# Top-10 indices of each row on one core: instruction order of the schedule versus program order, stores on another queue, loads in four pieces

## The chip, the core and the metric

The kernel runs on one core of one Trainium2 chip. Five instruction streams work on that core side by side: TensorE (not used here), VectorE (DVE in the profile), ScalarE (ACT), GpSimd (POOL) and SyncE (SP). The metric is device time in microseconds, from launch to completion; lower is better. The kernel before has a median of 1136.94 us over 3 runs (1134.1 to 1137.37).

## The reference

For every row of an 8192 x 8192 fp32 matrix it gives the column indices of the 10 largest values, the largest first:

```python
def reference(x, k):                       # x: (8192, 8192) float32, k = 10
    indices = np.argpartition(x, -k, axis=1)[:, -k:]
    values = np.take_along_axis(x, indices, axis=1)
    sorted_idx = np.argsort(-values, axis=1)
    return np.take_along_axis(indices, sorted_idx, axis=1)
```

The matrix is 268 MB and every byte must be read once. The output is 8192 x 10 64-bit integers.

## The kernel before

The rows are cut into 64 tiles of 128 rows, one row in each of the 128 partitions. A row is seen as 256 chunks of 32 values. A tile goes through three stages.

- `load(t)` (L70): SP's queue brings the tile's 4 MB into one of four `xt` buffers, in two DMAs of half the columns each (eight for tile 0).
- `front(t)` (L81): DVE takes the maximum of each chunk (`reduce_max`, L87, one instruction for 8192 elements per partition), then the 8 largest chunk maxima (`max`, L117), their chunk numbers (`max_index`, L118, into `cid`), strikes them out (`match_replace`, L120) and repeats for the next 8 (L122, L123). The 10 largest values of a row lie in the 10 chunks with the largest maxima. So these 10 chunks are fetched again from the matrix in HBM: ACT turns chunk numbers into row offsets (`off`, L104: 8 of them, then 2), and POOL issues 10 indirect DMAs (L109), each of which gathers one chunk of 32 values for all 128 rows into `g`.
- `back(t)` (L127): DVE finds the top 16 among the 320 gathered values with the same five kinds of instruction (L133 to L137) and leaves their positions in `pos`. The first of them, L133, reads all of `g`, and so waits for all 10 gathers. Every eighth tile `decode` (L141) turns the positions of 8 tiles into column indices (six DVE instructions) and stores 80 KB by a DMA on SP's queue (L165).

`cid`, `pos` and the decode's buffers are kept for a batch of `TB = 8` tiles. The buffers of the pool `small` (`m`, `w16`, `m2`, `off`, `g`, ...) rotate over `LAG + 2 = 4` places.

Each engine runs its instructions in the order in which the build put them, and starts one when its semaphores allow it; nothing behind a waiting instruction passes it. What sets that order is the framework's scheduler: it takes the program's dependences and its own cost estimates and may place instructions of different stages between each other. The loop as it is written (L170) calls `load(t)`, `front(t)`, `back(t - 2)` in turn, but the order on DVE is the scheduler's.

Of the kernel before, what the change touches and what calls it, by code (L numbers as in the profile page):

```python
# [10 lines left out]
P = 128  # L11
N = 8192
C = 32
NCHUNK = N // C
KMAX = 10
G = 10
TB = 8
BIG_NEG = -1e30
LAG = 2


@with_exitstack
def kernel(
    ctx: ExitStack,
    tc: tile.TileContext,
    x: bass.AP,
    k: bass.AP,
    out: bass.AP,
):
    nc = tc.nc  # L30
    assert isinstance(k, int) and k == KMAX, f"only k=10 supported, got {k}"
    nrows, rowlen = x.shape
    assert rowlen == N and nrows % (P * TB) == 0, (nrows, rowlen)
    ntiles = nrows // P

    fp32 = mybir.dt.float32
    fp16 = mybir.dt.float16
    u16 = mybir.dt.uint16
    u32 = mybir.dt.uint32
    i32 = mybir.dt.int32  # L40
    X_AX = mybir.AxisListType.X
    ALU = mybir.AluOpType
    ACTF = mybir.ActivationFunctionType

    out_u32 = out.bitcast(u32)
    out_tpn = out_u32.rearrange("(t p) n -> p t n", p=P)

    x_chunks = x.rearrange("r (c w) -> (r c) w", w=C)

    consts = ctx.enter_context(tc.tile_pool(name="consts", bufs=1))  # L50
    xpool = ctx.enter_context(tc.tile_pool(name="x", bufs=4))
    small = ctx.enter_context(tc.tile_pool(name="small", bufs=LAG + 2))
    bpool = ctx.enter_context(tc.tile_pool(name="batch", bufs=2))

    rowbase = consts.tile([P, 1], i32)
    nc.gpsimd.iota(rowbase, pattern=[[0, 1]], base=0, channel_multiplier=NCHUNK)
    rowbase_f = consts.tile([P, 1], fp32)
    nc.vector.tensor_copy(out=rowbase_f, in_=rowbase)
    slots_i = consts.tile([P, G], i32)
    nc.gpsimd.iota(slots_i, pattern=[[1, G]], base=0, channel_multiplier=0)  # L60
    slots = consts.tile([P, G], fp16)
    nc.vector.tensor_copy(out=slots, in_=slots_i)
    opacks = [consts.tile([P, TB, KMAX, 2], u32, name=f"opack{i}") for i in range(2)]
    for o in opacks:
        nc.gpsimd.memset(o, 0)

    st = {}
    batch = {}

    def load(t):  # L70
        xt = xpool.tile([P, N], fp32, tag="xt")
        r0 = t * P
        nparts = 8 if t == 0 else 2
        w = N // nparts
        for h in range(nparts):
            nc.sync.dma_start(
                out=xt[:, h * w:(h + 1) * w], in_=x[r0:r0 + P, h * w:(h + 1) * w]
            )
        st[t] = {"xt": xt}

    def front(t):  # L81
        xt = st[t]["xt"]
        m = small.tile([P, NCHUNK], fp32, tag="m")
        nparts = 8 if t == 0 else 1
        w = N // nparts
        for h in range(nparts):
            nc.vector.reduce_max(  # L87
                out=m[:, h * w // C:(h + 1) * w // C],
                in_=xt[:, h * w:(h + 1) * w].rearrange("p (c w) -> p c w", w=C),
                axis=X_AX,  # L90
            )
        if t % TB == 0:
            batch[t // TB] = (
                bpool.tile([P, TB, 16], u32, tag="cidb", name="cidb"),
                bpool.tile([P, TB, 16], u32, tag="posb", name="posb"),
            )
        cid = batch[t // TB][0][:, t % TB, :]
        w16 = small.tile([P, 16], fp32, tag="w16")
        m2 = small.tile([P, NCHUNK], fp32, tag="m2")
        off = small.tile([P, G], i32, tag="off")  # L100
        g = small.tile([P, G * C], fp32, tag="g")

        def gather(lo, hi):
            nc.scalar.activation(  # L104
                out=off[:, lo:hi], in_=cid[:, lo:hi], func=ACTF.Identity,
                bias=rowbase_f[:, 0:1], scale=1.0,
            )
            for s in range(lo, hi):
                nc.gpsimd.indirect_dma_start(  # L109
                    out=g[:, s * C:(s + 1) * C],  # L110
                    out_offset=None,
                    in_=x_chunks,
                    in_offset=bass.IndirectOffsetOnAxis(ap=off[:, s:s + 1], axis=0),
                    element_offset=t * P * N,
                )

        nc.vector.max(out=w16[:, 0:8], in_=m)  # L117
        nc.vector.max_index(out=cid[:, 0:8], in_max=w16[:, 0:8], in_values=m)  # L118
        gather(0, 8)
        nc.vector.match_replace(out=m2, in_to_replace=w16[:, 0:8], in_values=m,  # L120
                                imm_value=BIG_NEG)
        nc.vector.max(out=w16[:, 8:16], in_=m2)  # L122
        nc.vector.max_index(out=cid[:, 8:16], in_max=w16[:, 8:16], in_values=m2)  # L123
        gather(8, G)
        st[t]["g"] = g

    def back(t):  # L127
        g = st.pop(t)["g"]
        pos = batch[t // TB][1][:, t % TB, :]
        t8a = small.tile([P, 8], fp32, tag="t8a")  # L130
        t8b = small.tile([P, 8], fp32, tag="t8b")
        g2 = small.tile([P, G * C], fp32, tag="g2")
        nc.vector.max(out=t8a, in_=g)  # L133
        nc.vector.max_index(out=pos[:, 0:8], in_max=t8a, in_values=g)  # L134
        nc.vector.match_replace(out=g2, in_to_replace=t8a, in_values=g, imm_value=BIG_NEG)  # L135
        nc.vector.max(out=t8b, in_=g2)  # L136
        nc.vector.max_index(out=pos[:, 8:16], in_max=t8b, in_values=g2)  # L137
        if t % TB == TB - 1:
            decode(t // TB)

    def decode(b):  # L141
        cidb, posb = batch.pop(b)
        slot = bpool.tile([P, TB, KMAX], u32, tag="slot")
        low = bpool.tile([P, TB, KMAX], u32, tag="low")
        nc.vector.tensor_scalar(out=slot, in0=posb[:, :, 0:KMAX], scalar1=C.bit_length() - 1,
                                scalar2=None, op0=ALU.logical_shift_right)
        nc.vector.tensor_scalar(out=low, in0=posb[:, :, 0:KMAX], scalar1=C - 1,
                                scalar2=None, op0=ALU.bitwise_and)
        shape = [P, TB, KMAX, G]
        hot = bpool.tile(shape, fp16, tag="hot")  # L150
        pick = bpool.tile([P, TB, KMAX], fp32, tag="pick")
        nc.vector.tensor_tensor(  # L152
            out=hot, in0=slot.unsqueeze(3).to_broadcast(shape),
            in1=slots.unsqueeze(1).unsqueeze(1).to_broadcast(shape), op=ALU.is_equal,
        )
        nc.vector.tensor_tensor(  # L156
            out=hot, in0=hot, in1=cidb[:, :, 0:G].unsqueeze(2).to_broadcast(shape),
            op=ALU.mult,
        )
        nc.vector.reduce_sum(out=pick, in_=hot, axis=X_AX)  # L160
        o = opacks[b % 2]
        nc.vector.scalar_tensor_tensor(
            out=o[:, :, :, 0], in0=pick, scalar=float(C), in1=low, op0=ALU.mult, op1=ALU.add,
        )
        nc.sync.dma_start(  # L165
            out=out_tpn[:, b * TB:(b + 1) * TB, :],
            in_=o.rearrange("p t k two -> p t (k two)"),
        )

    for t in range(ntiles):  # L170
        load(t)
        front(t)
        if t >= LAG:
            back(t - LAG)
    for t in range(ntiles - LAG, ntiles):
        back(t)


# [33 lines left out]
```

## Time and profile before

| what | value |
|---|---|
| median of 3 runs | 1136.94 us (1134.1 to 1137.37) |
| the profiled execution's own time | 1134.35 us |
| span of its instructions | 1132.6 us |
| DVE busy | 842.8 us (74%) |
| POOL busy | 614.4 us (54%) |
| ACT busy | 39.4 us (3%) |
| moved by DMA | 279.81 MB, mean 247 GB/s over the span |

The time of an execution is 1.75 us more than the span of its instructions. The page gives for each group of instructions its busy time, the mean of one, and the idle time of its engine just before it with what ended that idle time. POOL's busy time is that of issuing gathers, not of their landing. A DMA's time to landing runs from its issue to the semaphore that its waiters see.

### The profile page before, as it was taken

The page shows a single profiled execution, that of the slowest core. Times are in us where ns is not written, and L with a number is a line of the kernel's source. Part 1 is how long each engine was busy: PE and PEld are TensorE (multiplying, and loading weights), DVE is VectorE, ACT ScalarE, POOL GpSimd, SP SyncE. Part 2 cuts the span into 40 slices and gives each one's busy share as a digit, 9 for nine tenths or more (in the row PEclk, how much of TensorE's full clock was granted, in tenths as well). Part 3 has the DMA queues.
Part 4 walks back from the last instruction along what each step waited for, and adds up shares of the span by engine and source line. Part 5 has one row for each costly group of instructions (what it writes and reads, how often), then busy time and mean ns, then how long its engine had stood idle before and what let it go on. Part 6 is the DMA issues. An engine that isn't in the chain of part 4 may idle for free.

```text
span 1132.6 us, 2913 instructions
## 1 busy us (share of the span) xinstructions
DVE 842.8 (74%) x1145; ACT 39.4 (3%) x129; POOL 614.4 (54%) x648
## 2 busy tenths in 40 slices
DVE  4747658786787876977769875778858787787883
ACT  0000000000000000000000000000000000000000
POOL 3244536654465645655547554575536663565663
DMA  9985550899319982399625996179950999329600
GB/s 383 419 340 217 176 210 11 317 408 363 138 24 389 407 334 84 90 409 406 250 82 169 407 408 228 26 255 409 361 203 11 344 409 362 112 30 407 265 11 10
DMA packets 48118, 279.81 MB, mean 247 GB/s; under 512 B 20704, under 2 KB 30944, under 8 KB 31968
## 3 DMA queue, kind: packets, MB, share of 16 engines
q1 hardware_dynamic: 27616, 269.10, 60.1%
q0 software_dynamic: 20480, 10.53, 4.7%
q14 instruction: 22, 0.18, 0.0%
HBM read 278.92 MB, written 0.66 MB: 247 GB/s over the span
## 4 chain that ended last, share of the span: by engine, by line
DMA 37%; POOL 25%; DVE 22%; issue 14%; ACT 1%; DVEq 0%; SPq 0%; POOLq 0%; ACTq 0%
DMA g<-in_x_dram,off 36%; POOL g L109 25%; DVE m L87 12%; DVE t8a L133 2%; DVE cidb L118 2%; DVE posb L134 1%; DVE w L117 1%; ACT off L104 1%; DMA xt<-in_x_dram 1%; DVE g L135 1%; DVE hot L156 1%; DVE pick L160 1%; DVE posb L137 1%; DVE t8b L136 1%; DVE cidb L123 0%
## 5 line engine op out<-in xcount | busy, mean ns | idle before, releaser
L109 POOL DMA_INDIRECT g<-in_x_dram,off x640 | 613.6, 959 | 505.7 <-ACT off L104 327.8
L87 DVE TENSOR_REDUCE m<-xt 128x256 f32<-128x8192 f32 (+1 forms) x71 | 555.9, 7829 | 4.8 <-DMA xt<-in_x_dram 4.5
L133 DVE MAX8 t8a<-g 128x8 f32<-128x320 f32 x64 | 31.5, 493 | 279.4 <-DMA g<-in_x_dram,off 228.9
L104 ACT ACTIVATE off<-cidb,rowbase_f 128x8 int32<-128x8 uint32 (+1 forms) x128 | 38.2, 298 | 1070.1 <-DVE cidb L118 767.5
L134 DVE FIND_INDEX8 posb<-t8a,g 128x8 uint32<-128x320 f32 x64 | 31.0, 485 | 0.0
L137 DVE FIND_INDEX8 posb<-t8b,g 128x8 uint32<-128x320 f32 x64 | 31.0, 484 | 0.0
L136 DVE MAX8 t8b<-g 128x8 f32<-128x320 f32 x64 | 30.7, 480 | 0.3
L135 DVE MATCH_REPLACE8 g<-t8a,g 128x320 f32<-128x320 f32 x64 | 30.4, 475 | 0.0
L118 DVE FIND_INDEX8 cidb<-w,m 128x8 uint32<-128x256 f32 x64 | 26.8, 418 | 0.0
L123 DVE FIND_INDEX8 cidb<-w,m 128x8 uint32<-128x256 f32 x64 | 26.8, 418 | 0.0
L122 DVE MAX8 w<-m 128x8 f32<-128x256 f32 x64 | 26.5, 414 | 0.1
L117 DVE MAX8 w<-m 128x8 f32<-128x256 f32 x64 | 26.3, 411 | 0.1
L120 DVE MATCH_REPLACE8 m<-w,m 128x256 f32<-128x256 f32 x64 | 26.1, 408 | 0.0
L152 DVE TENSOR_TENSOR hot<-slot,slots 128x800 f16<-128x800 uint32 x8 | 7.9, 992 | 0.0
L156 DVE TENSOR_TENSOR hot<-hot,cidb 128x800 f16<-128x800 f16 x8 | 7.9, 982 | 0.0
L160 DVE TENSOR_REDUCE pick<-hot 128x80 f32<-128x800 f16 x8 | 7.8, 970 | 0.0
L134 DVE MATCH_VALUE_LOAD posb<-t8a,g 128x8 f32 x64 | 4.9, 77 | 0.3
L137 DVE MATCH_VALUE_LOAD posb<-t8b,g 128x8 f32 x64 | 4.9, 76 | 0.3
L135 DVE MATCH_VALUE_LOAD g<-t8a,g 128x8 f32 x64 | 4.9, 77 | 0.0
L118 DVE MATCH_VALUE_LOAD cidb<-w,m 128x8 f32 x64 | 4.8, 75 | 0.1
L123 DVE MATCH_VALUE_LOAD cidb<-w,m 128x8 f32 x64 | 4.7, 74 | 0.1
L120 DVE MATCH_VALUE_LOAD m<-w,m 128x8 f32 x64 | 4.6, 72 | 0.0
(13 smaller groups left out, 10.1 us busy)
## 6 DMA issues: line engine op xcount, KB each, us to landing
xt<-in_x_dram SPq DMA_DIRECT2D x126, 2048.0 KB, 18.0
g<-in_x_dram,off POOLq DMA_INDIRECT x640, 6.0
xt<-in_x_dram SPq DMA_DIRECT2D x8, 512.0 KB, 6.6
out_dram<-opack SPq DMA_DIRECT2D x8, 80.0 KB, 3.8
```

The lines of the kernel that those rows point to most:

```text
L87: nc.vector.reduce_max(out=m[:, h * w // C:(h + 1) * w // C], in_=xt[:, h * w:(h + 1) * w].rearrange("p (c w) -> p c w", w=C), axis=X_AX,)
L104: nc.scalar.activation(out=off[:, lo:hi], in_=cid[:, lo:hi], func=ACTF.Identity, bias=rowbase_f[:, 0:1], scale=1.0,)
L109: nc.gpsimd.indirect_dma_start(out=g[:, s * C:(s + 1) * C], out_offset=None, in_=x_chunks, in_offset=bass.IndirectOffsetOnAxis(ap=off[:, s ...
L117: nc.vector.max(out=w16[:, 0:8], in_=m)
L118: nc.vector.max_index(out=cid[:, 0:8], in_max=w16[:, 0:8], in_values=m)
L120: nc.vector.match_replace(out=m2, in_to_replace=w16[:, 0:8], in_values=m, imm_value=BIG_NEG)
L123: nc.vector.max_index(out=cid[:, 8:16], in_max=w16[:, 8:16], in_values=m2)
L133: nc.vector.max(out=t8a, in_=g)
L134: nc.vector.max_index(out=pos[:, 0:8], in_max=t8a, in_values=g)
L135: nc.vector.match_replace(out=g2, in_to_replace=t8a, in_values=g, imm_value=BIG_NEG)
L136: nc.vector.max(out=t8b, in_=g2)
L137: nc.vector.max_index(out=pos[:, 8:16], in_max=t8b, in_values=g2)
```

## The change

Four things are edited.

1. The loop is wrapped in `tc.manual_schedule()`: each engine's instructions stay in the order in which the program issues them. The loop is rewritten so that three tiles are loaded ahead and iteration t does `front(t)`, `load(t + 3)`, `rank(t - 2)` (`rank` is the old `back`).
2. The result store moves from SP's queue to ACT's queue.
3. A tile is loaded in four DMAs (1 MB each) instead of two, and the chunk maxima are taken by two `reduce_max` of 4096 elements instead of one of 8192 (tile 0 keeps its eight and eight).
4. The pool `small` has `LAG + 1 = 3` places instead of 4.

All the other instructions, their shapes and their number are the same.

```diff
-    small = ctx.enter_context(tc.tile_pool(name="small", bufs=LAG + 2))
+    small = ctx.enter_context(tc.tile_pool(name="small", bufs=LAG + 1))
...
     def load(t):
-        xt = xpool.tile([P, N], fp32, tag="xt")
+        xts[t] = xpool.tile([P, N], fp32, tag="xt", name="xt")
         r0 = t * P
-        nparts = 8 if t == 0 else 2
+        nparts = 8 if t == 0 else 4
...
     def front(t):
-        xt = st[t]["xt"]
+        xt = xts.pop(t)
         m = small.tile([P, NCHUNK], fp32, tag="m")
-        nparts = 8 if t == 0 else 1
+        nparts = 8 if t == 0 else 2
...
-        nc.sync.dma_start(
+        nc.scalar.dma_start(
             out=out_tpn[:, b * TB:(b + 1) * TB, :],
...
-    for t in range(ntiles):
-        load(t)
-        front(t)
-        if t >= LAG:
-            back(t - LAG)
-    for t in range(ntiles - LAG, ntiles):
-        back(t)
+    with tc.manual_schedule():
+        for t in range(3):
+            load(t)
+        for t in range(ntiles + LAG):
+            if t < ntiles:
+                front(t)
+                if t + 3 < ntiles:
+                    load(t + 3)
+            if t >= LAG:
+                rank(t - LAG)
```

The first place is DVE at tile 2, in the order before. The numbers behind the names are the program's: `m_149` are the chunk maxima of tile 2, `g_128` is the gathered data of tile 1 (tile 0's is `g_102`).

```order
L87 TENSOR_REDUCE m_149<-xt_146 128x256
L133 MAX t8a_206<-g_128 128x8
L117 MAX w16_151<-m_149 128x8
L134 MAX_INDEX posb_98<-t8a_206,g_128 128x8
L118 MAX_INDEX cidb_97<-w16_151,m_149 128x8
L120 MATCH_REPLACE m2_152<-w16_151,m_149 128x256
L135 MATCH_REPLACE g2_208<-t8a_206,g_128 128x320
L122 MAX w16_151<-m2_152 128x8
L136 MAX t8b_207<-g2_208 128x8
L123 MAX_INDEX cidb_97<-w16_151,m2_152 128x8
L137 MAX_INDEX posb_98<-t8b_207,g2_208 128x8
```

The same place on DVE in the changed kernel; here `m_166` are the chunk maxima of tile 2 and `g_114` is the gathered data of tile 0.

```order
L85 TENSOR_REDUCE m_166<-xt_95 128x128 x2
L115 MAX w16_169<-m_166 128x8
L116 MAX_INDEX cidb_109<-w16_169,m_166 128x8
L118 MATCH_REPLACE m2_170<-w16_169,m_166 128x256
L120 MAX w16_169<-m2_170 128x8
L121 MAX_INDEX cidb_109<-w16_169,m2_170 128x8
L130 MAX t8a_195<-g_114 128x8
L131 MAX_INDEX posb_110<-t8a_195,g_114 128x8
L132 MATCH_REPLACE g2_197<-t8a_195,g_114 128x320
L133 MAX t8b_196<-g2_197 128x8
L134 MAX_INDEX posb_110<-t8b_196,g2_197 128x8
```

Before, the ranking of tile 1 began right behind the chunk maxima of tile 2, ahead of the chunk numbers of tile 2 (L118), and the two stages alternated. Now the chunk numbers of tile 2 (L116) come first, all five instructions of a stage stand together, and the tile that is ranked is tile 0, one tile further back.

The second place is SP's queue around a store, in the order before.

```order
L76 DMA xt_716<-in_x_dram 128x4096 x2
L76 DMA xt_750<-in_x_dram 128x4096
L165 DMA out_0_dram<-opack1_76 128x8x20
L76 DMA xt_750<-in_x_dram 128x4096
L76 DMA xt_784<-in_x_dram 128x4096 x2
```

In the changed kernel the same store stands on ACT's queue, between the offsets of two tiles (it is the store of the first batch that is shown).

```order
L102 ACTIVATE off_432<-cidb_391,rowbase_f_69 128x8
L102 ACTIVATE off_432<-cidb_391,rowbase_f_69 128x2
L162 DMA out_0_dram<-opack0_75 128x8x20
L102 ACTIVATE off_480<-cidb_391,rowbase_f_69 128x8
L102 ACTIVATE off_480<-cidb_391,rowbase_f_69 128x2
```

SP's queue now holds loads alone; on ACT's queue the store is followed by the offsets of the next tile.

More of the change, by code (lines that the diff above doesn't have):

```diff
@@ L65 @@
         nc.gpsimd.memset(o, 0)
-    st = {}
-    batch = {}
+    xts, cids, gs, batch = {}, {}, {}, {}
     def load(t):
-        xt = xpool.tile([P, N], fp32, tag="xt")
+        xts[t] = xpool.tile([P, N], fp32, tag="xt", name="xt")
         r0 = t * P
-        nparts = 8 if t == 0 else 2
+        nparts = 8 if t == 0 else 4
         w = N // nparts
@@ L76, in load @@
             nc.sync.dma_start(
-                out=xt[:, h * w:(h + 1) * w], in_=x[r0:r0 + P, h * w:(h + 1) * w]
+                out=xts[t][:, h * w:(h + 1) * w], in_=x[r0:r0 + P, h * w:(h + 1) * w]
             )
-        st[t] = {"xt": xt}
     def front(t):
-        xt = st[t]["xt"]
+        xt = xts.pop(t)
         m = small.tile([P, NCHUNK], fp32, tag="m")
-        nparts = 8 if t == 0 else 1
+        nparts = 8 if t == 0 else 2
         w = N // nparts
@@ L100, in front @@
         off = small.tile([P, G], i32, tag="off")
-        g = small.tile([P, G * C], fp32, tag="g")
+        gs[t] = small.tile([P, G * C], fp32, tag="g", name="g")
         def gather(lo, hi):
@@ L109, in gather @@
                 nc.gpsimd.indirect_dma_start(
-                    out=g[:, s * C:(s + 1) * C],
+                    out=gs[t][:, s * C:(s + 1) * C],
                     out_offset=None,
```

5 lines of the change are left out of this document (2 added, 3 removed).

## The prediction

> **What bounds the kernel now.** I read the page first: the span, the busy shares, the queues and the groups of instructions.
>
> ```profile
> span 1132.6 us, 2913 instructions
> DVE 842.8 (74%) x1145; ACT 39.4 (3%) x129; POOL 614.4 (54%) x648
> q1 hardware_dynamic: 27616, 269.10, 60.1%
> q0 software_dynamic: 20480, 10.53, 4.7%
> L109 POOL DMA_INDIRECT g<-in_x_dram,off x640 | 613.6, 959 | 505.7 <-ACT off L104 327.8
> ```
>
> No resource is full. DVE has most work, 842.8 us, and sits idle for 289.8 us. So the second view is what DVE and SP's queue waited for.
>
> ```profile
> DVE t8a L133 <- DMA g<-in_x_dram,off: 228.9, 36, 17.1
> DVE t8a L133 <- issue: 50.5, 14, 6.8
> DVE m L87 <- DMA xt<-in_x_dram: 4.5, 2, 4.4
> SPq L76 <- DVE m L87: 665.8, 46, 21.9
> SPq L165 <- DVE w L122: 287.7, 7, 41.3
> ```
>
> 279.4 of DVE's 289.8 us stand before one instruction, L133, the first of a ranking, which needs all ten gathers. (The 50.5 us put down to "issue" stand before the same instruction; I take them as the same wait.) For a loaded tile DVE waited 4.5 us in all. SP's queue stood 41 us at a time behind a store, and that reached nobody. Third, the timeline of two tiles in the first batch:
>
> ```profile
> 85.37 0.49 DVE L133 MAX8 t8a<-g 128x8 f32<-128x320 f32 x1 [7.82 <-DMA g<-in_x_dram,off]
> 85.78 0.41 DVE L117 MAX8 w<-m 128x8 f32<-128x256 f32 x1
> 87.65 0.94 POOL L109 DMA_INDIRECT g<-in_x_dram,off  x1 [8.32 <-ACT off L104]
> 89.39 8.67 DVE L87 TENSOR_REDUCE m<-xt 128x256 f32<-128x8192 f32 x1
> 98.89 0.94 POOL L109 DMA_INDIRECT g<-in_x_dram,off  x1 [0.30 <-issue]
> 105.70 0.49 DVE L133 MAX8 t8a<-g 128x8 f32<-128x320 f32 x1 [7.64 <-DMA g<-in_x_dram,off]
> ```
>
> This is a loop through three engines: ranking of one tile (85.37), chunk numbers of the next right behind it, ten gathers (87.65 to 98.89, one each 1.25 us), their landing, and only then the next ranking (105.70): 20.3 us, of which DVE waits 7.6. The schedule lets DVE run only one tile ahead of its gathers, with the next chunk numbers queued behind the waiting instruction.
>
> **The change part by part.**
>
> *The order, what it removes.* In the new order the ranking of tile t-2 stands behind all of `front(t)`. From the end of a tile's first chunk numbers to its ranking lie two whole periods and the rest of a front. Whether this is enough: the last tile's rows show the chain undisturbed, and the chain of waits its slowest landing.
>
> ```profile
> 1107.53 0.42 DVE L118 FIND_INDEX8 cidb<-w,m 128x8 uint32<-128x256 f32 x1
> 1119.84 0.95 POOL L109 DMA_INDIRECT g<-in_x_dram,off  x1 [0.30 <-issue]
> 1122.37 0.49 DVE L133 MAX8 t8a<-g 128x8 f32<-128x320 f32 x1 [11.99 <-DMA g<-in_x_dram,off]
> 212.90 8.54 DMA g<-in_x_dram,off
> ```
>
> From 1107.95 to the last gather's issue are 11.9 us; the landing is 2.5 us with no loads running and 8.54 us at the worst among those I looked at, so 14.4 to 20.5 us. The new distance is two periods and 1.29 us of front, 2 x 13.62 + 1.29 = 28.5 us (both worked out below). Slack 8 us: every wait at L133 goes except at the end. POOL needs 10 x 1.25 = 12.5 us per tile and is next in line if the period falls below that.
>
> *The order, what it adds.* The alternation hid something. A DVE instruction that needs its predecessor's result starts after it; one that doesn't starts earlier. Tiles 0 and 1 ran unmixed:
>
> ```profile
> 34.11 0.49 DVE L133 MAX8 t8a<-g 128x8 f32<-128x320 f32 x1 [17.11 <-DMA g<-in_x_dram,off]
> 34.64 0.09 DVE L134 MATCH_VALUE_LOAD posb<-t8a,g 128x8 f32 x1
> 36.70 8.67 DVE L87 TENSOR_REDUCE m<-xt 128x256 f32<-128x8192 f32 x1
> 45.40 0.43 DVE L117 MAX8 w<-m 128x8 f32<-128x256 f32 x1
> 45.94 0.42 DVE L118 FIND_INDEX8 cidb<-w,m 128x8 uint32<-128x256 f32 x1
> 47.65 8.67 DVE L87 TENSOR_REDUCE m<-xt 128x256 f32<-128x8192 f32 x1
> ```
>
> Ranking alone: 36.70 - 34.11 = 2.59 us. Front behind the reduce: 47.65 - 45.40 = 2.25. Together 4.84; the mixed form took 89.39 - 85.37 = 4.02. So each tile pays 0.82 us for the order. Reduce: 45.40 - 36.70 = 8.70. Period with one reduce: 8.70 + 2.25 + 2.59 = 13.54 us. (A behaviour of DVE that the trace shows: 85.78 starts 0.08 us before 85.37's end, 34.64 starts 0.04 after 34.11's end.) [...]
>
> *Two reduces for one.*
>
> ```profile
> L87 DVE TENSOR_REDUCE m<-xt 128x256 f32<-128x8192 f32 x63 | 546.1, 8669 | 0.0
> L87 DVE TENSOR_REDUCE m<-xt 128x32 f32<-128x1024 f32 x8 | 9.8, 1220 | 4.8 <-DMA xt<-in_x_dram 4.5
> ```
>
> (8669 - 1220) / 7168 = 1.039 ns per element, so 156 ns fixed. The second half pays it once more, and as it needs nothing of the first, 0.08 us overlaps: +0.08 us, period 13.62. Bounds: 0 to 0.16 us per tile, 0 to 10 us in all. It gains only at tile 1, where a half can be reduced while the other lands.
>
> *Four pieces and the store's queue.* DVE waited 4.5 us for tiles, all at the start; 60.1% + 4.7% of the span is 734 us of DMA work, 11.5 us per tile against 13.62. So these edits are worth nothing to the middle. The cover is the four buffers; without it a tile costs its 10.5 us of transfer. The store on ACT costs about what it cost SP, 0.40 us:
>
> ```profile
> 200.32 0.40 SPq L165 DMA_DIRECT2D out_dram<-opack  x1
> 66.58 0.30 ACT L104 ACTIVATE off<-cidb,rowbase_f 128x8 int32<-128x8 uint32 x1 [18.51 <-DVE cidb L118]
> ```
>
> It waits for the decode's last DVE instruction. Behind it on ACT stand the next tile's offsets, which need chunk numbers that DVE makes 9 us after that decode: nobody waits. Bounds 0 to 0.4 us for each of 8. If it did not hide, POOL's gathers would be late next, into the 8 us of slack.
>
> *Three places for four* in `small`: a place used by tile t was last used by tile t-3, whose ranking stands before `front(t)` on DVE. No new wait; 0.
>
> *The waits of L130.* It waits on eight gather semaphores, as L133 did:
>
> ```profile
> L133 DVEq EVENT_SEMAPHORE  x256: 21/50/11918, 27.8 to 1122.3; - x128
> 200.21 0.42 DVE L122 MAX8 w<-m 128x8 f32<-128x256 f32 x1
> 200.55 0.49 DVE L133 MAX8 t8a<-g 128x8 f32<-128x320 f32 x1
> ```
>
> Four wait instructions of 50 ns each. Where the gathers had landed (200.55) they hid behind the running instruction. I take 0; the other end is 0.2 us x 62 = 12 us.
>
> *The sum*, on the profiled execution's clock:
>
> ```profile
> 4.19 9.21 DMA xt<-in_x_dram
> 16.59 0.42 DVE L123 FIND_INDEX8 cidb<-w,m 128x8 uint32<-128x256 f32 x1
> 1125.07 0.20 DVE L145 TENSOR_SCALAR slot<-posb 128x80 uint32<-128x80 uint32 x1
> 1128.38 0.24 DVE L162 SCALAR_TENSOR_TENSOR opack<-pick,low 128x80 uint32<-128x80 f32 x1
> ```
>
> - Start. Tile 0 has landed at 13.40 and its front ends at 17.0. The last 7 of its 8 pieces took 9.21, so a tile takes 10.5; tile 1 lands at 23.9. Half a reduce (4.4) and 2.25 more: `front(2)` begins at 30.5.
> - Tiles 2 to 63, each with a ranking: 62 x 13.62 = 844.4.
> - Seven decodes on DVE between them, now unmixed: 1128.62 - 1125.07 = 3.55 each, 24.9. This ends at 899.8.
> - Tail. Tile 63's first chunk numbers came 2.59 + 1.29 us (from 46.36 to 47.65) earlier, at 895.9; 14.4 us on, at 910.3, its gathers are there; tile 62's ranking has long ended. From L133 at 1122.37 to the end of the span were 10.2 us: 920.5.
>
> With the 1.75 us around the span 922.3 us, against 1134.35 for the profiled execution. That execution lies at the low end of the runs (1134.1 to 1137.37), their median 2.6 us above it; so a little above 922: I say 923. From the other side: 1132.6 - 279.4 (all waits at L133) + 62 x 0.90 + 2.4 (tile 1) + 8.5 (tail) = 920.
>
> **The rivals.**
>
> 1. *The order costs no DVE time.* Then the 0.82 us stay hidden and the period is 12.8, just above POOL's 12.5: 923 - 62 x 0.82 = 872 us. [...] Chance 0.07.
> 2. *Gathers become the bound.* A gather waits until the one eight before it has landed (eight completion semaphores). Loads now run without the long pauses of before, so landings may lengthen. The interval is the larger of 1.25 us and landing/8; POOL decides from 1.36 us, a landing of 10.9. Time is about 640 x interval + 30 us (16 at the start, 2.5 landing, 10.2 at the end, 1.75 around): at a landing of 13 us it is 1070; it is slower than before from 13.8, and at 14.5 gives 1190. For it: landings of 6 us in the middle, 2.5 with no loads, 8.54 under loads, so loads do lengthen them. Against it: the 8.54 came in the densest stretch of loads, and POOL kept 1.25 us there. Slower than before 0.03; between 945 and 1130, 0.08. The Trainium skill ("DMA: Bandwidth & Descriptors", section "Queues, rings and completion order") says that the DMA engines change queue at each packet; rows of 8 KB instead of 16 KB would then shorten landings under load. No run here shows that yet.
> 3. *The order isn't what mattered*, DVE's wait turning up elsewhere with the same length: 1137. Against it: the new order leaves 28.5 us where 20.5 are needed. Chance 0.02.
>
> **How the numbers follow.** The forecast, DVE bound all through the middle, has 0.80: 923 us. Its own unknowns are -5 to +5 for the split, up to +12 for L130's waits, a few us for the start and decodes: 912 to 943. The range goes to 905 on the side of rival 1, for half hidden costs, and to 945: 2 in 10 are left out. Faster by over 0.3% (the least that a measurement of this kernel tells from no change): 0.80 + 0.07 + 0.08 = 0.95; within 0.3%: 0.02; slower: 0.03.
>
> **What would show it.** Right: DVE busy over 93% of the span at about 860 us or more, idle time before L130 under 25 us instead of 279 and nearly all at the end; `front` to `front` 13.6 us; gathers 1.25 us apart with a pause of about 1 us per tile; SP waiting for DVE and never for a store. Wrong: L130 waiting in the middle (rival 2, with gathers further apart), a period near 12.8 (rival 1), or DVE waiting before L85 for tiles, which would mean that the pieces cost bandwidth.

## The result and the profile after

| kernel | median us | runs | ratio to before, 95% interval |
|---|---|---|---|
| before | 1136.26 | 4, 1134.1 to 1137.37 | 1 |
| changed, first measurement | 932.64 | 4, 928.6 to 943.31 | 0.820 [0.816, 0.824] |
| changed, second measurement | 921.99 | 4, 921.84 to 922.32 | 0.8126 [0.8112, 0.8139] |

The ratio of the first measurement leaves out its run of 943.31 us, which is over 1.5% above the fastest; that of the second is to the kernel before run beside it, 1135.16 us. The change takes 18 to 19% off the time. The forecast was 923 us between 905 and 945. The same kernel was measured twice because its first profile held something that the forecast had no place for (below); the second time it ran as worked out. The page of the first measurement, its span, busy shares and queues:

```profile
span 932.9 us, 3191 instructions
DVE 883.5 (95%) x1208; ACT 39.4 (4%) x129; POOL 610.0 (65%) x648
q1 hardware_dynamic: 37440, 268.45, 73.0%
q0 software_dynamic: 20480, 10.53, 5.9%
```

DVE is now busy 95% of the span. Its busy time rose by 41 us against the kernel before. Some 37 us of that come with the unmixed order (the kernel with program order and one reduce, below, has 879.6), some 4 us with the second reduce. The unmixed order costs short gaps besides, so its whole price is larger; the mixed kernel below measures it. What DVE waited for in the same run:

```profile
DVE t8a L130 <- DMA g<-in_x_dram,off: 8.1, 2, 7.9
DVE m L85 <- DMA xt<-in_x_dram: 6.9, 3, 4.6
DVE t8b L133 <- remote: 4.5, 2, 2.5
DVE t8b L133 <- issue: 2.5, 1, 2.5
DVE hot L153 <- remote: 1.8, 1, 1.8
```

The 279.4 us before the first instruction of a ranking have become 8.6 us, 7.9 of them at the very end. The last three rows are new. The timeline shows where such a wait stands: between two steps of the ranking of tile 1, both on DVE, with nothing from outside to wait for.

```profile
56.18 0.47 DVE L132 MATCH_REPLACE8 g<-t8a,g 128x320 f32<-128x320 f32 x1
59.11 0.49 DVE L133 MAX8 t8b<-g 128x8 f32<-128x320 f32 x1 [2.45 <-issue]
```

In the second measurement there are none of these. Its span on the page:

```profile
span 920.3 us, 3191 instructions
```

And its groups of waits, with all of DVE's longer than 0.5 us:

```profile
DVE t8a L130 <- DMA g<-in_x_dram,off: 8.0, 2, 7.8
DVE m L85 <- DMA xt<-in_x_dram: 6.9, 3, 4.6
```

The idle times in question add up to some 12.5 us in the first measurement, the spans differ by 12.6. The steady middle is the same in both. One period of the second by its timeline, with the last row a first gather of the next tile and POOL's pause before it:

```profile
98.45 8.73 DVE L85 TENSOR_REDUCE m<-xt 128x128 f32<-128x4096 f32 x2
107.21 0.43 DVE L115 MAX8 w<-m 128x8 f32<-128x256 f32 x1
109.46 0.47 DVE L130 MAX8 t8a<-g 128x8 f32<-128x320 f32 x1
112.03 8.73 DVE L85 TENSOR_REDUCE m<-xt 128x128 f32<-128x4096 f32 x2
122.40 0.94 POOL L107 DMA_INDIRECT g<-in_x_dram,off  x1 [1.41 <-ACT off L102]
```

Reduce to reduce are 13.58 us, and POOL pauses 1.4 us before a tile's first gather, where it paused 8.3 us in the stretch of the kernel before that the prediction shows. DVE sets the period.

### The profile page after: what moved, and what is told of

Same layout as the page of the kernel before. It is cut to its first block, busy times and chain, and to the rows that moved or that the text cites. A ratio compares the mean times of both kernels' runs of the same rounds, so it can differ in the third digit from the quotient of the medians.

```text
span 932.9 us, 3191 instructions
## 1 busy us (share of the span) xinstructions
DVE 883.5 (95%) x1208; ACT 39.4 (4%) x129; POOL 610.0 (65%) x648
## 4 chain that ended last, share of the span: by engine, by line
DVE 48%; DMA 19%; POOL 16%; issue 14%; ACTq 1%; ACT 1%; SPq 0%; another core or an unknown queue 0%; DVEq 0%; POOLq 0%
DVE m L85 32%; POOL g L107 16%; DMA g<-in_x_dram,off 12%; DMA xt<-in_x_dram 7%; DVE posb L131 2%; DVE t8b L133 2%; DVE t8a L130 2%; DVE g L132 2%; DVE cidb L116 2%; DVE w L115 2%; ACTq L102 1%; DVE pick L157 1%; DVE hot L153 1%; DVE hot L149 1%; DVE posb L134 1%
## 5 line engine op out<-in xcount | busy, mean ns | idle before, releaser
L85 DVE TENSOR_REDUCE m<-xt 128x128 f32<-128x4096 f32 (+1 forms) x134 | 559.7, 4215 | 7.2 <-DMA xt<-in_x_dram 6.9
L133 DVE MAX8 t8b<-g 128x8 f32<-128x320 f32 x64 | 31.7, 495 | 9.0 <-remote 4.5
L130 DVE MAX8 t8a<-g 128x8 f32<-128x320 f32 x64 | 30.5, 476 | 8.6 <-DMA g<-in_x_dram,off 8.1
L132 DVE MATCH_REPLACE8 g<-t8a,g 128x320 f32<-128x320 f32 x64 | 30.5, 476 | 0.0
L120 DVE MAX8 w<-m 128x8 f32<-128x256 f32 x64 | 27.4, 428 | 2.2
L115 DVE MAX8 w<-m 128x8 f32<-128x256 f32 x64 | 27.4, 428 | 2.2
L116 DVE FIND_INDEX8 cidb<-w,m 128x8 uint32<-128x256 f32 x64 | 26.8, 419 | 0.0
L118 DVE MATCH_REPLACE8 m<-w,m 128x256 f32<-128x256 f32 x64 | 26.2, 409 | 0.0
L116 DVE MATCH_VALUE_LOAD cidb<-w,m 128x8 f32 x64 | 5.9, 92 | 2.6
L121 DVE MATCH_VALUE_LOAD cidb<-w,m 128x8 f32 x64 | 5.9, 92 | 2.3 <-DVE w L120 0.2
L118 DVE MATCH_VALUE_LOAD m<-w,m 128x8 f32 x64 | 4.6, 72 | 0.0
```

The costliest lines, as they stand in the source:

```text
L85: nc.vector.reduce_max(out=m[:, h * w // C:(h + 1) * w // C], in_=xt[:, h * w:(h + 1) * w].rearrange("p (c w) -> p c w", w=C), axis=X_AX,)
```

## The experiments

All times are medians; the kernel before ran beside each at 1132 to 1135 us.

### The changed kernel once more

No edit: the file of the first measurement, on another occasion, beside other kernels.

> The changed kernel itself once more, beside the others. The profile of it showed 12.5 us of idle time on DVE in the middle, before instructions that wait only for DVE itself (2.5, 2.5, 2.0, 1.8 us and smaller), and its runs were apart by 15 us; with the store on SP's queue there was none of this and the time was 922.2 us. Theory A (it comes with the store on ACT's queue): 928 to 940 us again with such stalls, runs apart by several us. Theory B (a disturbance of that chip or those runs, not of the program): 921 to 924 us, no stalls, runs within 1 us.

Measured 921.99 us (921.84 to 922.32), with the profile shown above: none of the idle times between DVE's own instructions, and a span 12.6 us shorter. For this kernel they belong to the occasion or the chip, not to the program alone. What sets them off is taken up again with the mixed kernels, and is not settled there.

### The store back on SP's queue

```diff
-        nc.scalar.dma_start(
+        nc.sync.dma_start(
             out=out_tpn[:, b * TB:(b + 1) * TB, :],
```

> The changed kernel with one edit undone: the result store is back on SP's queue, in program order behind the loads of three tiles ahead. My theory (the period is DVE's own instructions, loads are three tiles ahead): the store holds back one load by about 8 us, which has more than two periods of slack; DVE's wait before L85 stays under 10 us in all and the time is that of the changed kernel, 926 to 938 us. Rival (taking the store off the load queue was part of the gain): seven or eight loads late by about 8 us each, DVE waits for tiles, 960 us or more.

Measured 922.23 us (922.2 to 922.25), 0.813 [0.812, 0.814] of before: the same as the changed kernel's 921.99. SP's queue stands behind the store, and DVE does not notice, as its groups of waits show (total, times, longest):

```profile
SPq L162 <- DVE opack L159: 212.7, 8, 74.1
DVE m L85 <- DMA xt<-in_x_dram: 6.7, 3, 4.5
```

In this program, moving the store is worth nothing. My theory holds.

### The fixed order undone

```diff
-    with tc.manual_schedule():
+    if True:
```

> The changed kernel with the fixed program order undone: the scheduler orders the instructions again; store on ACT's queue, four pieces, two reduces, three places and the loop with loads three ahead all stay. My theory (the order alone made the gain): the ranking stands again one tile behind and ahead of the next chunk numbers, a loop of about 20 us through DVE, POOL and the gathers' landing in most tiles; 1100 to 1150 us with 250 us or more of waits before L130. Rival (the other edits carry part of it): below 1050 us.

Measured 928.38 us in one run. My expectation was wrong by 170 us: the change does not need the fixed order for most of its gain. The busy time on its page says a part of why:

```profile
DVE 841.2 (91%) x1208; ACT 39.4 (4%) x129; POOL 608.3 (66%) x648
```

Its groups of waits say the rest:

```profile
DVE t8a L130 <- DMA g<-in_x_dram,off: 66.0, 9, 10.4
DVE t8a L130 <- issue: 7.1, 1, 7.1
```

73 us of waits instead of 279. The built order differs from that of the kernel before, although the scheduler made both: a ranking stands ahead of the next tile's chunk numbers for 10 tiles of 64 (the first eight, one more, and the last, which has no next tile), where before it was 36. The scheduler had answered to the other edits. It keeps the mixed form, so its DVE is busy 42 us less than in the fixed order and has 15 us less of gaps too short for this view, and it pays 65 us more in waits before L130.

### Four pieces alone

The kernel before with nothing but this edit, the scheduler still at work:

```diff
-        nparts = 8 if t == 0 else 2
+        nparts = 8 if t == 0 else 4
...
-        nparts = 8 if t == 0 else 1
+        nparts = 8 if t == 0 else 2
```

> The kernel before with one edit alone: loads in four pieces and two reduces of half a tile, the scheduler still ordering; store on SP's queue, old loop, four places. Built, its order on DVE has the ranking of the last tile ahead of the next chunk numbers in 16 tiles instead of 36. Theory C (the time follows the order that the scheduler makes, and the other edits act through it): 36 such tiles cost 250 us before, about 7 us each, so 16 cost about 115 us, 960 to 990 us. Rival (fixed program order is needed for the gain): 1100 us or more. Rival (pieces act as pieces, by earlier data): no fewer waits before L133 per such tile, but DVE's waits before L87, 5 us in all, fall.

Measured 962.12 us, 0.848 [0.846, 0.849] of before. In its built order 17 tiles are ranked ahead of the next chunk numbers, the last one included. Its waits:

```profile
DVE t8a L133 <- DMA g<-in_x_dram,off: 90.9, 20, 10.5
DVE t8a L133 <- issue: 11.9, 2, 7.2
DVE m L87 <- DMA xt<-in_x_dram: 6.6, 3, 4.4
```

These are 102.8 us, where the kernel above has 73.1 and the kernel before 279.4. By the timelines, 83.5 of the 102.8 us stand at those 17 tiles, 68.8 of the 73.1 at the 10 tiles of the kernel above, and 203.1 of the 279.4 at the 36 of the kernel before: 5 to 7 us each, in three kernels. The rest stands at tiles whose ranking comes behind the next chunk numbers, but only 0.4 to 2 us behind them (14 tiles before, 4 to 7 us each); that distance is too short for the gathers as well. The rival in my expectation that counts on earlier data does not hold: DVE waits no less for its loads than before. So the edit acts through the order that the scheduler makes of it, not as a better transfer. This is the strongest support that the place of the ranking is what costs.

### Program order alone

The kernel before, its loop as it was, with `tc.manual_schedule()` around it and nothing else.

```diff
-    for t in range(ntiles):
-        load(t)
-        front(t)
-        if t >= LAG:
-            back(t - LAG)
-    for t in range(ntiles - LAG, ntiles):
-        back(t)
+    with tc.manual_schedule():
+        for t in range(ntiles):
+            load(t)
+            front(t)
+            if t >= LAG:
+                back(t - LAG)
+        for t in range(ntiles - LAG, ntiles):
+            back(t)
```

> The kernel before with one edit alone: program order kept, nothing else (one load call ahead of each front, store on SP's queue, two pieces, one reduce, four places). My theory: the middle has the same period of 13.55 us, but each of the first seven stores now stands on SP's queue ahead of the next tile's load and waits for the decode, so that the tile behind it is loaded only after it: DVE waits 11 to 12 us for it, 7 times, about 80 us. 933 - 5 (one reduce) + 80 = 1005 us, between 985 and 1020, and about 80 us of waits for xt before L87. Rival (order is all there is to it, the loads' place and the store's queue are worth nothing): 925 to 935 us.

Measured 1031.12 us, 0.909 [0.907, 0.910] of before; above my interval. The mechanism is as I said, its price was too low. A store and the first reduce behind it, in the timeline:

```profile
146.91 0.40 SPq L165 DMA_DIRECT2D out_dram<-opack  x1
162.81 8.69 DVE L87 TENSOR_REDUCE m<-xt 128x256 f32<-128x8192 f32 x1 [15.92 <-DMA xt<-in_x_dram]
176.35 8.67 DVE L87 TENSOR_REDUCE m<-xt 128x256 f32<-128x8192 f32 x1
```

The sum of such waits, in the groups of waits:

```profile
DVE m L87 <- DMA xt<-in_x_dram: 119.0, 9, 15.9
```

The wait is 15.9 us where I took 11 to 12. From 147.4, when the loads behind the store were issued, to 162.8 the queues moved 4.95 MB at a mean of 322 GB/s, with little in the first microseconds; a tile is 4.19 MB, and the rate I had used came from a stream that was running. The period, 13.54 us with one reduce, is that of the prediction.

### Program order and the store on ACT

The same, with the store on ACT's queue as the one further edit.

```diff
-        nc.sync.dma_start(
+        nc.scalar.dma_start(
             out=out_tpn[:, b * TB:(b + 1) * TB, :],
```

> The kernel before with two edits: program order kept, and the store on ACT's queue (old loop with one load call ahead of each front, two pieces, one reduce, four places). With the store on SP this order cost 119 us of waits for xt before L87, 15 to 16 us behind each of seven stores. Theory (only the store stood in the loads' way; SP runs ahead of the loop as far as the four buffers allow, wherever the load call stands in the text): these waits go but for 11 us at the start, 1031 - 108 = 923 us, between 917 and 927. Rival (the loads have to be called three tiles ahead as well): 960 us or more, with waits for xt left.

Measured 922.46 us (922.29 to 922.63), 0.8135 [0.812, 0.815]. The 108 us are gone from the groups of waits:

```profile
DVE m L87 <- DMA xt<-in_x_dram: 11.1, 2, 6.6
DVE t8a L133 <- DMA g<-in_x_dram,off: 8.0, 2, 7.8
```

So a fixed order needs one of two things for its loads: calls three tiles ahead of the store (as with the store put back on SP, 922.23), or a queue without the store. The change has both, and one is spare. Three small places for four, loads called three tiles ahead, four pieces and two reduces together add nothing to these two edits: 922.46 against 921.99. (The reduces do two things that cancel: DVE waits 11.1 us for its first loads with one, 6.9 with two, and the period is 13.53 us with one, 13.58 with two.)

### One tile between chunk numbers and ranking

```diff
-LAG = 2
+LAG = 1
```

> The changed kernel with LAG = 1: program order, but rank(t-1) behind front(t), so one period instead of two between a tile's chunk numbers and its ranking (the pool small follows with two places). My theory: the distance needed is 11.9 us to the last gather's issue plus a landing of 3 to 6 us; the period is that sum less the 1.29 us of front behind the chunk numbers, 13.6 to 16.6 us, so 930 to 1110 us, most likely near 1010, with a wait before L130 in nearly every tile. Rival (the place of the ranking behind the whole front is what counts, not the distance in tiles): 922 to 935 us without waits.

Measured 942.94 us in one run: below my likeliest, near the rival's figure. The sum of DVE's waits at L130, in its groups of waits:

```profile
DVE t8a L130 <- DMA g<-in_x_dram,off: 25.5, 8, 10.4
```

By the timeline, 12.5 of the 25.5 us are five waits of up to 2.9 us in the first 170 us, 2.6 us are two waits later on, and 10.4 us stand at the last tile, where the changed kernel has 7.8. In most tiles there is no wait. There the timeline shows the first eight chunk numbers of a tile, its last gather and its ranking:

```profile
308.00 0.42 DVE L116 FIND_INDEX8 cidb<-w,m 128x8 uint32<-128x256 f32 x1
320.30 0.94 POOL L107 DMA_INDIRECT g<-in_x_dram,off  x1 [0.30 <-issue]
323.30 0.47 DVE L130 MAX8 t8a<-g 128x8 f32<-128x320 f32 x1
```

From the end of these chunk numbers (308.42) to the ranking are 14.9 us, and that is just enough: the last gather, issued at 320.30, had landed within 3 us. I had reckoned with landings of 3 to 6. In the steady state the next load starts when a reduce ends and takes about as long as the first eight gathers do, so the last ones meet quiet DMA engines; that explanation fits the timing but was not tested by itself. What counts is that the ranking stands behind the chunk numbers; the second tile of distance takes away these short waits, most of them at the start, and is worth 21 us by this one run.

### The same order, mixed by hand

`front` and `rank` become generators that yield after each step, and each iteration alternates them, `front` first:

```diff
+    def mix(*gens):
+        gens = list(gens)
+        while gens:
+            for g in list(gens):
+                try:
+                    next(g)
+                except StopIteration:
+                    gens.remove(g)
...
+            parts = []
...
-                front(t)
-                if t + 3 < ntiles:
-                    load(t + 3)
+                parts.append(front(t))
...
-                rank(t - LAG)
+                parts.append(rank(t - LAG))
+            mix(*parts)
+            if t + 3 < ntiles:
+                load(t + 3)
```

> The changed kernel with the instructions of front(t) and of rank(t-2) alternating on DVE, written out by hand, front first; everything else the same. My theory (a DVE instruction that does not need its predecessor's result starts 0.08 us before that one ends, one that needs it 0.04 us after): 0.82 us less for each of 62 tiles, a period of 12.76 us, 933 - 51 = 882 us, between 872 and 892; POOL's 12.5 us per tile is then close to the bound. Rival (the rule that the pipe is drained between any two DVE instructions): 925 to 938 us, the period unchanged.

Measured 875.34 us (875.15 to 875.41), 0.772 [0.770, 0.773] of before, the fastest kernel of this study. Its busy shares:

```profile
DVE 849.1 (97%) x1208; ACT 39.4 (5%) x129; POOL 609.7 (70%) x648
```

And one period of its timeline:

```profile
303.71 0.43 DVE L115 MAX8 w<-m 128x8 f32<-128x256 f32 x1
304.08 0.49 DVE L135 MAX8 t8a<-g 128x8 f32<-128x320 f32 x1
307.78 8.72 DVE L85 TENSOR_REDUCE m<-xt 128x128 f32<-128x4096 f32 x2
316.54 0.43 DVE L115 MAX8 w<-m 128x8 f32<-128x256 f32 x1
```

The period is 12.83 us (316.54 - 303.71) against 13.58: 0.75 us per tile, 47 us in all, with the same instructions on DVE. The second starts 0.06 us before the first ends (304.08 against 304.14). The rival, a pipe that is drained between any two DVE instructions, gave 925 to 938 us; the measurement decides against it for these instructions. The Trainium skill ("VectorE: DVE Perf Modes", section "The DRAIN you can't avoid") has the next instruction wait until the pipe is empty, but says beside it that one that is not held starts earlier. The trace agrees with the second half, by these 0.06 us.

### One reduce or two in the mixed order

Three kernels: one reduce of 8192 elements from tile 1 on, halves for tile 1 only, halves for tiles 1 to 3.

```diff
-        nparts = 8 if t == 0 else 2
+        nparts = 8 if t == 0 else 1
...
+        nparts = 8 if t == 0 else 2 if t == 1 else 1
...
+        nparts = 8 if t == 0 else 2 if t <= 3 else 1
```

> The hand-mixed order of front(t) and rank(t-2) with one reduce of 8192 elements for two of 4096. My theory: one instruction less per tile, 0.08 us, 62 times: 5 us less than the mixed kernel with two reduces (875.3 us), so 869 to 872 us. Rival (halves let DVE start on the first half while the second lands): slower than 875 us, with more waiting before the reduce.

> The hand-mixed order with two half reduces for tile 1 alone and one reduce from tile 2 on. Theory (two reduces cost 0.06 us per tile in the middle, 3.8 us in all, and gain 4 us once, at tile 1, where the first half is reduced while the second lands): both gains together, 871 to 872.5 us. Rival (the two mixed kernels differ by something else): 874 us or more.

> The hand-mixed order with two half reduces for tiles 1 to 3 and one reduce from tile 4 on. With halves for tile 1 alone the 4 us came back at tile 2, whose chunk numbers came 15.5 us after tile 1's instead of 11.3: DVE waited for tile 2 to land in full. Theory (halves gain while DVE is ahead of the first loads, up to tile 3, and cost 0.06 us per tile from there): 875.3 - 60 x 0.06 = 871.7 us, between 871 and 872.5. Rival (the 4 us are lost at whichever tile first has one reduce): 875.5 us or more.

One reduce: 876.74 us, not 870. Halves for tile 1: 876.69, not 872. Both expectations fell, and the groups of the former say half of the reason:

```profile
L85 DVE TENSOR_REDUCE m<-xt 128x256 f32<-128x8192 f32 x63 | 546.1, 8669 | 6.7 <-DMA xt<-in_x_dram 6.7
```

In the middle one reduce is better as expected, 12.77 against 12.83 us per tile, 4 us in all. At the start it loses as much: DVE is then faster than the loads, and the first tile with one reduce must land in full (tile 2's chunk numbers came 15.5 us after tile 1's with halves for tile 1 only, 11.3 us with halves throughout). With halves for tile 1 only, the timeline has this wait at tile 2:

```profile
34.52 8.69 DVE L85 TENSOR_REDUCE m<-xt 128x256 f32<-128x8192 f32 x1 [4.14 <-DMA xt<-in_x_dram]
```

Halves for the first three tiles should have kept both gains. In that kernel tile 4 is the first with one reduce, and it did not wait for its load:

```profile
57.09 8.67 DVE L85 TENSOR_REDUCE m<-xt 128x256 f32<-128x8192 f32 x1
```

So the rival (the 4 us are lost at whichever tile first has one reduce) does not hold. But the kernel took 978.18 us (973.7 to 983.55) in place of 871.7, and not for any reason of this sum. Two of its groups of waits:

```profile
DVE slot L151 <- issue: 15.8, 3, 5.7
DVE w L123 <- remote: 12.8, 4, 5.0
```

One of these waits in its timeline:

```profile
268.67 0.20 DVE L151 TENSOR_SCALAR slot<-posb 128x80 uint32<-128x80 uint32 x1 [5.04 <-issue]
```

DVE idles in the same way as in the changed kernel's first measurement, up to 5.7 us at a time, before instructions that wait for DVE's own results alone. The same program was therefore run once more:

> The same kernel as the mixed order with halves for tiles 1 to 3, once more. It took 978 us, with idle time of up to 5 us on DVE before instructions that wait only for DVE itself, as in the first measurement of the changed kernel, which did not show in its second. Theory D (a disturbance from outside that time): 871 to 872.5 us without such idle time, as worked out before. Theory E (it belongs to this program): 970 to 985 us again, at the same tiles.

Measured 950.25 us (942.47 to 972.03) on another chip, with such idle times at mostly the same tiles (5, 9, 15, 23, 30, 34, 38, 42, 47, 54 and 63 come late in both). So here it is not an accident of one chip; theory E is nearer, though the size varies. Its first chip had run the mixed kernel with two reduces, and the changed kernel with the store on SP, without a trace of it. Whether halves for three tiles would give 871.7 us stays open.

## Why the prediction was right

- **The bound.** Right. Of the 279.4 us at L133, 203.1 came from a ranking that stood ahead of the next chunk numbers, in 36 tiles. The other 76 are of a kind that the prediction did not tell apart, as it showed only the first batch: the ranking stood behind the next chunk numbers, but right behind them. The new distance removes both. Three orders with 36, 17 and 10 tiles of the first kind waited 279, 103 and 73 us in all; the changed order, where only the last tile is left, 8.5.
- **Start.** 30.5 us was predicted for the start of `front(2)`; the second tile's half reduces ended as worked out and it began at 30.53 in both measurements.
- **Period.** 13.62 predicted, 13.58 measured. The 0.82 us for the unmixed order measured 0.75 (13.58 against 12.83 with all else the same); the split 0.08 predicted, 0.06 measured (12.83 against 12.77). The four wait instructions before L130 cost nothing, as taken.
- **Decodes.** 3.55 predicted, 3.60 measured (17.18 us for a tile with a decode).
- **Tail.** 14.4 us from tile 63's chunk numbers to its ranking, measured 14.3. The span came to 920.3 where 920.5 was worked out.
- **Four pieces, store, three places "worth nothing to the middle".** Right in program order (922.23 and 922.46 us without one or the other). But as a statement on the change it was too narrow: under the scheduler the same edits alter the order, four pieces alone bringing 962 us and all edits but the fixed order 928. Most of the gain has two causes in this change, either of which is enough: the fixed order with the loads' way kept free, or the other edits with the scheduler at work (one run). The third rival, that the order was not what mattered, was right to be small, but it does not follow that fixing the order is the only way to the gain.
- **Slack.** I said 28.5 us where up to 20.5 are needed. With 14.9 us (LAG = 1) most tiles did not wait, and the longest wait before the last tile was 2.9 us, so the need is about 15 in most tiles and 17.8 at the most. The 8.54 us landing, taken from a stretch in which loads caught up, was the wrong row for the middle. It was a bound on the safe side.
- **Rival 2, gathers as the bound.** Did not come: gathers stayed 1.25 us apart. Their median landing is 5.5 us with rows of 8 KB (with rows of 16 KB it is 6.0 before, and in program order 6.1 with the store on SP and 5.8 with it on ACT). The Trainium skill's rule on packets ("DMA: Bandwidth & Descriptors", section "Queues, rings and completion order") points this way; the difference is too small here to confirm it.
- **Rival 1, a free order.** Refuted: the period is 13.58 us and not 12.8, and the mixed kernel is 47 us faster with the same instructions.
- **What was not foreseen.** The first measurement's 12.5 us of idle time on DVE. The forecast of 923 was met by the second measurement, and missed by 10 us by the first.

## What to carry to other kernels

Read idle time before a consumer as a loop: if the instruction that waits for a gather stands ahead of the one that starts the next gather on the same in-order engine, their latencies add up in every turn, and swapping the two removes the wait, if what then lies between them is longer than the latency (14.9 us left short waits here, 28.5 next to none). Fixing the order by hand also takes away what a scheduler did well; alternate independent chains on the engine and keep the waiting chain second. Before you credit an edit, run it alone, since a piece size or a queue can change what the scheduler makes of everything else, and with a fixed order look at what each queue has behind a store.

## What the runs showed that was not expected

DVE can stand idle between two of its own dependent instructions. In the changed kernel's first measurement it was 12.5 us in all at three places; in its second, none. In the mixed kernel with halves for three tiles it was some 104 us in one profile and 65 in the next (the sums of the groups of waits, without those for loads and gathers), at mostly the same tiles, and none in the three other mixed kernels (875.15 to 875.41 us in four runs of one). Within such a place, one wait follows another, as the timeline of the first profile of that kernel shows:

```profile
508.94 0.49 DVE L141 MAX8 t8b<-g 128x8 f32<-128x320 f32 x1 [2.37 <-remote]
510.34 0.09 DVE L125 MATCH_VALUE_LOAD cidb<-w,m 128x8 f32 x1 [0.91 <-DVE t8b L141]
511.04 0.09 DVE L143 MATCH_VALUE_LOAD posb<-t8b,g 128x8 f32 x1 [0.21 <-DVE cidb L125]
```

The lengths repeat, as 0.2, 0.9, 1.6, 2.4 and 5.0 us. The instructions that are hit need a result that DVE itself has made just before. The match-and-replace steps, whose inputs the chunk-number or position step before them has already used, are hit only once (L139 in the second profile, 0.4 us). The DMA traffic gives no rule: in the first profile of that kernel it was 248 GB/s in the 2 us stretches that touch a wait of 0.8 us or more and 304 in the others, in the changed kernel's first measurement 377 against 314. Of the 24 transfers of the instruction queue in that first profile, 5 fell into such stretches, where chance would give 3 or 4. The cause is open. The profile of the kernel before has no such wait, and its runs of one occasion lie within 0.3% of each other.
